# Feed-forward tiles of a two-layer decoder trunk placed at 192 instead of 64 bytes (mod 256) behind the weights

## The chip, the core and the metric

The kernel runs on one core of a Trainium2 chip. The core has a matrix engine (TensorE, PE in the profile, with PEld for the load of a matmul's stationary operand), a vector engine (VectorE, DVE), a scalar engine (ScalarE, ACT), GpSimd (POOL), and SyncE (SP), which here issues the DMAs. Tiles live in SBUF, 128 partitions wide; matmul results go to PSUM. The metric is the device time in microseconds of one execution of the whole program; lower is better. A matmul has a stationary operand, 128 x 128 here, that is loaded beforehand, and a moving operand of up to 512 columns that is streamed past it. The load for the next matmul runs while the present one streams.

## The reference

Two layers, each a mixer and a dense feed-forward part, with RMSNorm before and after each sub-layer. 256 positions, width 2048, hidden width 8192, float32. Cut to what the change is near:

```python
def squared_relu_mlp(h, w_up, w_down):
    return jnp.square(jax.nn.relu(h @ w_up)) @ w_down

def reference(x, norm_w, ...):
    h = x
    for layer in range(DEPTH):                       # 2
        y = rmsnorm(h, norm_w[layer, 0])
        y = linear_attention_mixer(y, ...) if layer % 2 == 0 else spatial_gating_mixer(y, ...)
        h = h + rmsnorm(y, norm_w[layer, 1])
        y = squared_relu_mlp(rmsnorm(h, norm_w[layer, 2]), ffn_w_up[layer], ffn_w_down[layer])
        h = h + rmsnorm(y, norm_w[layer, 3])
    return h
```

The first mixer is a gated DeltaNet beside a retention, the second a chunked gMLP (spatial gating).

## The kernel before

**Products in three parts.** Every large product is made with operands split into a high part (float32r) and a low part, the rest. `weights` (from L126 on) takes a 128 x 2048 tile of weights by DMA into `raw`, copies it to `whi` on ScalarE (L136) and writes the rest to `wlo` on VectorE (L137). Each product of a 128 x 128 block is then three matmuls: high x high, low x high, high x low.

**Who is stationary.** In `prod_tok` (L140, matmuls at L143 to L145) the activations are stationary and the weights move, 512 columns as a rule. In `up_pass` (L319, matmuls at L330 to L332) it is the other way round: a 128 x 128 piece of the weights is stationary and 256 columns of the normed activations, `xh` and `xl`, move. In `chunk7` (L361, matmuls at L374 to L376) the activations are stationary again and 256 columns of weights move.

**The feed-forward stage.** `ffn` (L389) runs twice, once per layer. The hidden width is cut into 16 chunks of 512. For chunk c the up projection is four quarters of 48 matmuls (`up_pass`, a generator that is advanced one quarter at a time); squared ReLU of the result is split into a pair of tiles `e` (high and low, 128 x 4 x 256 each), and sums and differences of its parts into a pair `f` (`sums`). Between the four quarters for chunk c, the down projection of chunk c-1 is done in four blocks, one for each 512 output columns, in the order of `ORDER` (L37): quarter, block 0, quarter, block 1, quarter, block 2, quarter, block 3. For c = 1 the order is `FIRST` (L38). A block (L439) for output columns 0 and 2 is done with seven products instead of eight (`chunk7`, a Strassen-like scheme, 42 matmuls of 256 columns with `e` and `f` stationary); block 1 is done so in every second pass and in the plain way in the others; block 3 is always plain. A plain block is 24 matmuls of 512 columns through `chunk_tok` and `prod_tok`, with `e` stationary. The first chunk (`first_chunk`) and the last one (`down_last`) are done by `prod_tok` too, the last one with `e` stationary. There are 15 passes in each of the two stages.

The tiles have two sets of names, `e0`, `f0` and `e1`, `f1`, used in turn by even and odd chunks; h and l at the end stand for high and low.

**Places.** The tile pools lie one behind the other in each partition of SBUF, and a tile's place follows from the sizes ahead of it. The tiles of `raw`, `whi` and `wlo` are 8192 bytes per partition each, and 128 bytes of padding ahead of them (`PAD0`, L33) put their start at 0 mod 256. The normed activations `xh` and `xl` are put at an offset within a larger tile (`group`, L206, with `X_IN` or `X_UP`, L34). In the trunk's mixers both start at 0 mod 256, in the feed-forward stages both at 64. The feed-forward tiles come from `pair` (L393): a filler of 64 bytes, the high tile of 4096 bytes, the low tile of 4096 bytes, a filler of 192 bytes. All other tiles of that pool are multiples of 256 bytes, so `e` and `f`, high and low, all start at 64 mod 256, and the slices that matmuls read start at multiples of 512 bytes behind that. The fillers are tiles of their own that GpSimd sets to zero once (`skip`, L114 to L116).

So in the two feed-forward stages, mod 256 bytes:

| block | matmuls | stationary operand | moving operand |
|---|---|---|---|
| quarter of the up projection (L330 to L332) | 48 of 256 columns | weights, at 0 | x, at 64 |
| seven-product block (L374 to L376) | 42 of 256 columns | e or f, at 64 | weights, at 0 |
| plain block (L143 to L145) | 24 of 512 columns | e, at 64 | weights, at 0 |

Elsewhere `prod_tok` has its stationary operand at 0, but for one pair of tiles in the first layer's output projection (`Um0`, `Um1`), which lies at 224; and in the first product of the first layer the moving slices are 400 columns, 1600 bytes, apart, so that slice j of a weight tile starts at 64 x j mod 256.

Of the kernel before, what the change touches and what calls it, by code (L numbers as in the profile page):

```python
# [96 lines left out]
def program(tc, nc, A, S):  # L97
# [16 lines left out]
    def skip(pool, n):  # L114
        uid[0] += 1
        G.memset(pool.tile([P, n // 4], F32, tag=f"skip{uid[0]}", name=f"skip{uid[0]}"), 0.0)  # L116

    def T(pool, shape, tag, dt=F32, bufs=None):
        uid[0] += 1
        kw = {} if bufs is None else {"bufs": bufs}  # L120
        return pool.tile(shape, dt, tag=tag, name=f"{tag}_{uid[0]}", **kw)
# [267 lines left out]
    def ffn(up, dn, X, rh, w1i, w0i):  # L389
        last = HID // 512 - 1  # L390
        with tc.tile_pool(name=f"ffn{w1i}", bufs=1, reuse_waits="tile") as fp:

            def pair(name):  # L393
                if name in seen:
                    return T(fp, [P, 4, SEQ], f"{name}h", F32R), T(fp, [P, 4, SEQ], f"{name}l", F32R)
                seen.add(name)
                skip(fp, 64)
                hi = T(fp, [P, 4, SEQ], f"{name}h", F32R)
                lo = T(fp, [P, 4, SEQ], f"{name}l", F32R)
                skip(fp, 192)  # L400
                return hi, lo

            seen = set()
# [11 lines left out]
            def sums(a, c):  # L415

                t = T(fp, [P, 1024], "tr")
                F = t.rearrange("p (i m t) -> p i m t", m=2, t=P)
                V.tensor_tensor(F[:, 0], a[1][0], a[1][1], ALU.subtract)
                V.tensor_tensor(F[:, 1], F[:, 0], a[0][0], ALU.subtract)  # L420
                V.tensor_tensor(F[:, 2], a[0][0], a[1][0], ALU.subtract)
                V.tensor_tensor(F[:, 3], F[:, 1], a[0][1], ALU.add)
                f = pair(f"f{c % 2}")
                split(f[0].rearrange("p a t -> p (a t)"), f[1].rearrange("p a t -> p (a t)"), t)
                return f

            def rows(c):
                return [c * 512 + j * P for j in range(4)]

            e = pair("e0")  # L430
            Y, kept = {}, [bank(acc, 512, "acc") for _ in range(2)]

# [50 lines left out]
            for c in range(1, last + 1):  # L483
                e2 = pair(f"e{c % 2}")
                if c == last:
                    w1 = row_load(rows_in(["f1h", "f1l"]), "nrow", w1i)
                ps = [bank(tpp, 512, "tp") for _ in range(2)]
                todo = up_pass(up, X, c, ps)
                order = ORDER if c > 1 else FIRST
                for n, o in enumerate(order):  # L490
                    if o is None:
                        next(todo)
                        if None not in order[n + 1 :]:
                            r = [relu2(p) for p in ps]
                            for i in range(2):
                                sl = slice(2 * i, 2 * i + 2)
                                split(e2[0][:, sl, :], e2[1][:, sl, :], r[i].rearrange("p (m t) -> p m t", t=SEQ))
                            if c < last:
                                a = [x.rearrange("p (m b t) -> p b m t", b=2, t=P) for x in r]
                                f2 = sums([[a[i][:, b] for i in range(2)] for b in range(2)], c)  # L500
                    else:
                        block(o, c - 1, e, f)
                e, f = e2, f2
# [668 lines left out]
```

## Time and profile before

| | us |
|---|---|
| median of 3 runs | 2483.79 (2483.1 to 2485.16) |
| the profiled execution | 2481.77 |
| its span, from the first to the last instruction | 2480.0 |
| first layer's mixer, about | 0 to 536 |
| first feed-forward stage, about | 536 to 1248 |
| gMLP mixer, about | 1248 to 1793 |
| second feed-forward stage, about | 1793 to 2480 |

A timeline row gives an instruction's start and duration in us. Matmuls overlap in the records: one of 256 columns is recorded with 278 ns on average while the next one starts long before that is over. The rate is read from the difference of two starts and the number of matmuls in between. An idle time stands only where the engine really had nothing to do. In the rows of the view by stretches, busy times of the engines stand in the order PE, PEld, DVE, ACT, POOL, each with the number of instructions.

### The profile page before, as it was taken

The numbers are of one execution on the slowest core, as the hardware profiler recorded it, in microseconds if no ns is written. First come the engines' busy times: TensorE is split into PE (matmuls) and PEld (weight loads), VectorE is DVE, ScalarE is ACT, GpSimd is POOL, SyncE is SP. The second block draws the span as 40 slices with busy tenths as digits, with TensorE's granted clock in tenths as the row PEclk, the third lists the DMA queues.
The fourth block names the chain that finished last, engine by engine and source line by source line (L and its number), as shares of the span: only waits on it lengthen the run. The fifth ranks groups of instructions, "written<-read, shape, count | busy, mean of one in ns | idle before, by whom it ended". The sixth has DMA issues, their size and how long they took to land.

```text
span 2480.0 us, 37131 instructions
## 1 busy us (share of the span) xinstructions
PE 2447.2 (99%) x15418; PEld 2191.0 (88%) x15418; DVE 1977.1 (80%) x2322; ACT 1261.5 (51%) x1266; POOL 185.4 (7%) x162
## 2 busy tenths in 40 slices
PE   9999999999999999999999999999999999999998
PEld 8878888879999999999878878888799999999997
DVE  6686855578898899889854596866888988988897
ACT  7655444455554555555553433333555546555553
POOL 0001201140000000000210120100400000000001
PEclk9999999999999999999999999999999999999999
DMA  8444545544555555555555555565445555555553
GB/s 315 158 164 141 192 161 177 207 170 179 212 188 194 214 202 190 188 207 216 193 215 187 186 202 201 200 221 203 153 170 206 202 187 216 194 194 194 204 208 133
DMA packets 81832, 480.17 MB, mean 194 GB/s; under 512 B 13696, under 2 KB 15872, under 8 KB 27392
## 3 DMA queue, kind: packets, MB, share of 16 engines
q1 hardware_dynamic: 81664, 477.80, 53.6%
q8 instruction: 121, 1.98, 0.3%
q14 instruction: 47, 0.39, 0.0%
HBM read 475.14 MB, written 2.62 MB: 193 GB/s over the span
## 4 chain that ended last, share of the span: by engine, by line
PE 46%; DVE 3%; POOL 1%; issue 1%; ACT 0%; DVEq 0%; POOLq 0%; ACTq 0%
PE acc L145 8%; PE acc L143 8%; PE acc L144 8%; PE tp L331 4%; PE tp L330 4%; PE tp L332 4%; PE acc L374 1%; PE acc L375 1%; PE acc L376 1%; PE mx L376 1%; PE mx L375 1%; PE mx L374 1%; DVE wlo L137 1%; DVE h L287 1%; PE mx L1082 1%
## 5 line engine op out<-in xcount | busy, mean ns | idle before, releaser
L137 DVE TENSOR_TENSOR wlo<-raw,whi 128x2048 fp32r<-128x2048 f32 (+3 forms) x366 | 825.2, 2257 | 254.0 <-ACT whi L136 249.7
L136 ACT ACTIVATE whi<-raw 128x2048 fp32r<-128x2048 f32 (+3 forms) x366 | 685.4, 1876 | 436.5 <-PE acc L144 274.7
L331 PE MATMUL tp<-xl,whi 128*128 128x256 f32 x1920 | 533.5, 278 | 0.0
L330 PE MATMUL tp<-xh,whi 128*128 128x256 f32 x1920 | 533.5, 278 | 0.0
L332 PE MATMUL tp<-xh,wlo 128*128 128x256 f32 x1920 | 533.3, 278 | 0.0
L143 PE MATMUL acc<-whi,xh 128*128 128x512 f32 (+3 forms) x1120 | 439.1, 392 | 3.5 <-ACT whi L136 3.5
L145 PE MATMUL acc<-wlo,xh 128*128 128x512 f32 (+3 forms) x1120 | 431.6, 387 | 1.3 <-DVE wlo L137 1.2
L144 PE MATMUL acc<-whi,xl 128*128 128x512 f32 (+3 forms) x1120 | 432.0, 386 | 0.0
L330 PEld LDWEIGHTS tp<-xh,whi 128*128 128x128 f32 x1920 | 360.6, 188 | 2.1
L331 PEld LDWEIGHTS tp<-xl,whi 128*128 128x128 f32 x1920 | 360.2, 188 | 1.9
L332 PEld LDWEIGHTS tp<-xh,wlo 128*128 128x128 f32 x1920 | 360.0, 188 | 0.0
L200 ACT ACTIVATE whi<-qsum 128x2048 fp32r<-128x2048 f32 x74 | 142.0, 1919 | 221.0 <-DVE qsum L355 210.8
L143 PEld LDWEIGHTS acc<-whi,xh 128*128 128x128 f32 x1120 | 211.0, 188 | 44.2 <-ACT whi L136 4.9
L145 PEld LDWEIGHTS acc<-wlo,xh 128*128 128x128 f32 x1120 | 210.5, 188 | 42.7 <-DVE wlo L137 2.4
L144 PEld LDWEIGHTS acc<-whi,xl 128*128 128x128 f32 x1120 | 211.0, 188 | 39.2 <-issue 1.0
L201 DVE TENSOR_TENSOR wlo<-qsum,whi 128x2048 fp32r<-128x2048 f32 x74 | 169.5, 2291 | 64.9 <-ACT whi L200 63.1
L200 ACT ACTIVATE whi<-raw 128x1536 fp32r<-128x1536 f32 x74 | 110.4, 1493 | 188.2 <-DMA raw<-dn 91.2
L201 DVE TENSOR_TENSOR wlo<-raw,whi 128x1536 fp32r<-128x1536 f32 x74 | 129.9, 1755 | 0.6 <-ACT whi L200 0.6
L446 DVE TENSOR_TENSOR y<-acc,y 128x512 f32<-128x512 f32 x136 | 92.4, 687 | 43.7 <-PE acc L376 43.7
L277 POOL TENSOR_TENSOR e0h<-y,f1h 128x512 f32<-128x512 f32 x8 | 13.1, 1653 | 1327.8 <-DVE y L275 1327.8
L145 PE MATMUL acc<-wlo,e0h 128*128 128x512 f32 x256 | 101.2, 395 | 0.0
L143 PE MATMUL acc<-whi,e0h 128*128 128x512 f32 x256 | 101.1, 395 | 0.0
(358 smaller groups left out, 4319.8 us busy)
## 6 DMA issues: line engine op xcount, KB each, us to landing
raw<-up SPq DMA_DIRECT2D x128, 1024.0 KB, 4.8
raw<-dn SPq DMA_DIRECT2D x128, 1024.0 KB, 4.8
raw<-sg_in SPq DMA_DIRECT2D x64, 1024.0 KB, 4.8
raw<-la_in SPq DMA_DIRECT2D x56, 1024.0 KB, 4.8
raw<-sg_out SPq DMA_DIRECT2D x32, 1024.0 KB, 4.8
raw<-la_out SPq DMA_DIRECT2D x16, 1024.0 KB, 4.7
raw<-la_in SPq DMA_DIRECT2D x4, 768.0 KB, 7.8
kq<-xT SPq DMA_DIRECT2D x8, 256.0 KB, 6.0
```

Of the source, the lines that this page charges most:

```text
L136: ACT.activation(a, r, AF.Copy)
L137: V.tensor_tensor(d, r, a.bitcast(F32), ALU.subtract)
L143: PE.matmul(ps, xh, wh, start=first, stop=False)
L144: PE.matmul(ps, xl, wh, start=False, stop=False)
L145: PE.matmul(ps, xh, wl, start=False, stop=last)
L200: ACT.activation(hi, src, AF.Copy)
L201: V.tensor_tensor(lo, src, hi.bitcast(F32), ALU.subtract)
L330: PE.matmul(out, wh[:, col], xh, start=k == 0 and m % 2 == 0, stop=False, skip_group_check=True)
L331: PE.matmul(out, wh[:, col], xl, start=False, stop=False, skip_group_check=True)
L332: PE.matmul(out, wl[:, col], xh, start=False, stop=k == NKT - 1, skip_group_check=True)
L374: PE.matmul(ps, x[k][0], wh, start=k == 0, stop=False, skip_group_check=True)
L446: V.tensor_tensor(Y[k, c], p, Y[k, c], ALU.add)
```

## The change

The two fillers of each pair swap their sizes. Each pair of tiles starts 128 bytes later within the same 8448 bytes, so `e` and `f` lie at 192 mod 256 instead of 64; everything behind a pair stays where it was. The normed activations stay at 64, the weights at 0. No instruction is added, removed or put elsewhere in an engine's order.

```diff
@@ pair, in ffn
                 seen.add(name)
-                skip(fp, 64)
+                skip(fp, 192)
                 hi = T(fp, [P, 4, SEQ], f"{name}h", F32R)
                 lo = T(fp, [P, 4, SEQ], f"{name}l", F32R)
-                skip(fp, 192)
+                skip(fp, 64)
                 return hi, lo
```

## The prediction

> **What bounds the kernel now.** I read the page's header and busy line first, then the slices, then the chain of work that ended last.
>
> ```profile
> span 2480.0 us, 37131 instructions
> PE 2447.2 (99%) x15418; PEld 2191.0 (88%) x15418; DVE 1977.1 (80%) x2322; ACT 1261.5 (51%) x1266; POOL 185.4 (7%) x162
> ...
> PEclk9999999999999999999999999999999999999999
> ...
> PE 46%; DVE 3%; POOL 1%; issue 1%; ACT 0%; DVEq 0%; POOLq 0%; ACTq 0%
> ```
>
> TensorE is busy 99% of the span, its granted clock never dips, and no other engine holds more than 3% of the chain. The busy time by stretches says the same of the two feed-forward stages, the only ones that the change touches:
>
> ```profile
> 700.00:900.00 200.00, 200.00 (x1592) 193.54 (x1591) 180.65 (x175) 106.50 (x78) 0.00 (x0) 1.00 0.55 196
> 2000.00:2200.00 200.00, 200.00 (x1560) 192.20 (x1559) 178.87 (x172) 108.77 (x85) 0.00 (x0) 1.00 0.54 194
> ```
>
> The columns after the stretch are its length, then busy time of PE, PEld, DVE, ACT and POOL, clock, DMA share, GB/s. PE is busy 200.00 of 200 us, VectorE 180.65. So only the rate at which matmuls follow one another can change here. A matmul's own duration doesn't show that rate, because matmuls overlap; the starts do. I therefore took the timeline of PE and read two whole passes of the feed-forward loop, where each block of matmuls begins (columns: start and duration in us, engine, line, operation, operands, shapes; in L374 and L143 the weights move and e is stationary, in L330 the weights are stationary and x moves):
>
> ```profile
> 700.91 0.29 PE L374 MATMUL acc<-whi,e1h 128*128 128x256 f32 x1
> 705.68 0.28 PE L330 MATMUL tp<-xh,whi 128*128 128x256 f32 x1
> 711.13 0.28 PE L374 MATMUL acc<-whi,e1h 128*128 128x256 f32 x1
> 716.08 0.28 PE L330 MATMUL tp<-xh,whi 128*128 128x256 f32 x1
> 721.73 0.28 PE L374 MATMUL acc<-whi,e1h 128*128 128x256 f32 x1
> 726.50 0.28 PE L330 MATMUL tp<-xh,whi 128*128 128x256 f32 x1
> 731.95 0.39 PE L143 MATMUL acc<-whi,e1h 128*128 128x512 f32 x1
> 737.53 0.28 PE L330 MATMUL tp<-xh,whi 128*128 128x256 f32 x1
> 743.19 0.29 PE L374 MATMUL acc<-whi,e0h 128*128 128x256 f32 x1
> 747.96 0.28 PE L330 MATMUL tp<-xh,whi 128*128 128x256 f32 x1
> 753.41 0.39 PE L143 MATMUL acc<-whi,e0h 128*128 128x512 f32 x1
> 759.00 0.28 PE L330 MATMUL tp<-xh,whi 128*128 128x256 f32 x1
> 764.65 0.29 PE L374 MATMUL acc<-whi,e0h 128*128 128x256 f32 x1
> 769.42 0.28 PE L330 MATMUL tp<-xh,whi 128*128 128x256 f32 x1
> 774.87 0.39 PE L143 MATMUL acc<-whi,e0h 128*128 128x512 f32 x1
> 780.46 0.28 PE L330 MATMUL tp<-xh,whi 128*128 128x256 f32 x1
> 786.11 0.29 PE L374 MATMUL acc<-whi,e1h 128*128 128x256 f32 x1
> ```
>
> An L330 block is a quarter of the up projection: 48 matmuls. An L374 block is a seven-product block: 42. An L143 block is an ordinary one with 512 columns: 24. Up blocks take either 5.45 us (705.68 to 711.13; 113.5 ns a matmul) or 5.65 us (716.08 to 721.73; 117.7 ns). Seven-product blocks take either 4.77 us (700.91 to 705.68; 113.6 ns) or 4.95 us (711.13 to 716.08; 117.9 ns). I call the two lengths short and long: 0.20 us apart for an up block, 0.18 us for a seven-product block. The 512-column block takes 5.58 us, 232.5 ns a matmul.
>
> The rows also give a rule of succession. After a 512-column block the up block is always long (737.53, 759.00, 780.46). A seven-product block takes the other length than the up block ahead of it: long up, short block (737.53, 743.19); short up, long block (705.68, 711.13). An up block keeps the length of the seven-product block ahead of it (711.13, 716.08). PE waits for nothing in there, so the two lengths are two ways in which the stream of moving columns and the load of the next stationary operand run beside each other, and something at the border passes one way on to the next block.
>
> **The change part by part.** Nothing is added to or taken from any engine's list: the memsets of 64 and 192 bytes swap places, no tile changes size, no DMA or wait moves. The memsets of all such fillers are this row, 1.3 us together on GpSimd, which is idle 93% of the span; that idle time hides them and I cost their swap at nothing (with no cover it couldn't exceed the 1.3 us):
>
> ```profile
> L116 POOL MEMSET skip<- 128x16 f32 (+2 forms) x18 | 1.3, 125 | 0.3 <-PE tp L219 0.3
> ```
>
> What moves is the place of e and f, read only as stationary operands. Call "relation" the place of the stationary operand less that of the moving one, mod 256 bytes. In an up block the weights (0) are stationary and x (64) moves: relation 192, unchanged. In the other two kinds e or f is stationary and the weights move: relation 64 now, 192 after. The single matmul at the border from up to block, with x moving while e is loaded, goes from relation 0 to 128; the one back stays at 0.
>
> *Term 1, the 512-column matmuls.* Their number comes from the groups kept apart by shape, one operation of three:
>
> ```profile
> L145 PE MATMUL acc<-wlo,e0h 128*128 128x512 f32 x256 | 101.2, 395 | 0.0
> L145 PE MATMUL acc<-wlo,e1h 128*128 128x512 f32 x176 | 69.3, 396 | 0.0
> ```
>
> (256 + 176) x 3 = 1296. Their cost at relation 192 isn't in this trace at 512 columns. The nearest rows are these. First the gMLP stage, relation 0, 24 matmuls; then a stationary tile that lies at 224, 11 matmuls; then matmuls of 400 columns in the first projection, where x is stationary at 0 and slice j of the weights begins at 64 x j, so that the relation is 192, then 128, then 64, six matmuls each (five counted of the last):
>
> ```profile
> 1306.54 0.39 PE L144 MATMUL acc<-whi,xl 128*128 128x512 f32 x1
> 1311.98 0.39 PE L144 MATMUL acc<-whi,xl 128*128 128x512 f32 x1
> ...
> 502.22 0.39 PE L143 MATMUL acc<-whi,Um 128*128 128x512 f32 x1
> 504.78 0.39 PE L145 MATMUL acc<-wlo,Um 128*128 128x512 f32 x1
> ...
> 23.03 0.34 PE L143 MATMUL acc<-whi,xh 128*128 128x400 f32 x1
> 24.12 0.34 PE L143 MATMUL acc<-whi,xh 128*128 128x400 f32 x1
> 25.22 0.34 PE L143 MATMUL acc<-whi,xh 128*128 128x400 f32 x1
> 26.14 0.34 PE L145 MATMUL acc<-wlo,xh 128*128 128x400 f32 x1
> ```
>
> Relation 0: 5.44 / 24 = 226.7 ns. Relation 224: 2.56 / 11 = 232.7 ns, as dear as the 232.5 of relation 64. At 400 columns: 1.09 / 6 = 181.7 ns at 192, 1.10 / 6 = 183.3 at 128, 0.92 / 5 = 184 at 64. The bounds are so from 0 (dear as now) to 232.5 - 226.7 = 5.8 ns saved, 7.5 us over 1296. I take the row that has the very relation, 184 - 181.7, about 2 ns: **-2.6 us**. I see no dearer relation among these rows than the present one, so the term gets no positive end.
>
> *Term 2, the lengths of the 256-column blocks.* Up blocks show that relation 192 has the same two lengths (113.5 and 117.7 ns) that relation 64 has in seven-product blocks (113.6 and 117.9). So I expect no new length, only another choice between the two, and that choice hangs on the border matmul, of which no row has relation 128 at 256 columns. The bounds come from counting. Each stage runs 15 passes, 7 pairs like the one above and a first pass; I count both stages as 15 pairs. A pair has 8 up blocks (4 long) and 5 seven-product blocks (1 long). All short: -(4 x 0.20 + 1 x 0.18) x 15 = -14.7 us. All long: +(4 x 0.20 + 4 x 0.18) x 15 = +22.8 us. Between these I take the count as it is, **0 us**: the levels mirror each other, and every row in which a 512-column block ends leads to the same long up block.
>
> *Sum.* -2.6 us on the profiled execution, 2481.77 us (span 2480.0 and 1.8 us around it): 2479.2. The median of the three runs is 2483.79, 2.0 us above the profiled one, so the forecast is 2483.79 - 2.6 = **2481.2 us**. What hides nothing: VectorE and ScalarE aren't late anywhere in these stretches, and 2.6 us spread over 1400 us of stages leaves VectorE's 90% as it is.
>
> **The rivals.**
>
> *Stuck long (slower).* With one relation throughout, the swap at the entry to the seven-product block may vanish. For: the swap occurs only where the relation changes from 192 to 64. Since each 512-column block leaves the long way behind, all blocks would then stay long until the next one, and the pass never gets out: 2483.79 + 22.8 - 2.6 = 2504.0 us. It decides from the first border matmul at relation 128: if an up block at 5.65 us is followed by a seven-product block at 4.95 us, this is it. Against: an undisturbed stream needn't hold its way over a border matmul with yet another relation.
>
> *Swap at the other border (slightly slower).* If what is passed on is a lag between the two streams, which the change of relation turns into the other length, then now the lag is kept on entry and turned over on return; without a change of relation the length would be kept on entry and swapped on return. The pass runs long up, long block, short up: up blocks as before, seven-product blocks 4 long of 5 for 1 of 5. 3 x 0.18 x 15 = +8.1, less 2.6: 2489.3 us. For: it needs no new behaviour at relation 128. Against: only two borders carry it.
>
> *Stuck short (faster).* As the first rival, but the 512-column block at its new relation leaves the short way behind: 2483.79 - 14.7 - 2.6 = 2466.5 us. Against: now it leaves the long way whichever way it was entered (from short at 726.50 and 747.96 alike), and the border behind it is unchanged.
>
> *Nothing at all.* The change may not touch the reads' rate: 2483.8 us. The rows speak against it, 226.7 against 232.5 ns for one shape with PE never idle, and only the place told apart. [...]
>
> **How the numbers follow.** Count as it is, term 1 alone (2481.2): 0.30. Swap at the other border (2489.3): 0.22. Stuck long (2504.0): 0.16. Stuck short (2466.5): 0.14. Nothing (2483.8): 0.08. Other mixes of lengths between the ends: 0.10. 0.2% is 5.0 us, about what a measurement of this kernel can tell from no change. Faster takes stuck short, a part of the forecast where term 1 comes nearer its far end of 7.5 us (0.10), and most of the mixes (0.08): 0.32. Slower takes stuck long, most of the other-border case (0.16; in the rest term 1 eats it below 5.0) and a little of the mixes (0.02): 0.34. Same: the remaining 0.34. Both signs are open. The forecast's own range is 2476 to 2484 by the ends of term 1; the range that should hold 8 times in 10 reaches from stuck short to stuck long, whose prices are exact if they come at all, since leaving either out would leave out a case whose chance I can't put far below the others': 2466 to 2505.
>
> **What would show it.** In the timeline of the changed kernel the same borders can be read. Term 1: a 512-column block from L143 to the next L330 should take about 5.53 us (5.58 less 24 x 2 ns). Term 2: up blocks 5.45 or 5.65, seven-product blocks 4.77 or 4.95, in the order of now. The gMLP stage and the first layer should keep their times. A third length (near 5.76 us for an up block, say) would make "no new length" wrong; a long seven-product block behind a long up block would show the swap gone; any growth of VectorE's or ScalarE's share on the chain would show that something else than PE's reads was touched.

## The result and the profile after

| | before | after |
|---|---|---|
| median of 3 runs, us | 2483.79 | 2502.56 (2499.51 to 2503.12) |
| ratio, with 95% interval | | 1.0071 [1.0057, 1.0085] |
| profiled execution, us | 2481.77 | 2499.51 |
| its span, us | 2480.0 | 2497.7 |

The change makes the kernel 0.7% slower. The forecast was 2481.2 us; the time lies near that of the first rival, *stuck long* (2504.0 us).

The page of the changed kernel shows nothing of it in its shares. These are its header, its busy line, the granted clock and the engines of the chain of waits:

```profile
span 2497.7 us, 37131 instructions
PE 2465.4 (99%) x15418; PEld 2213.8 (89%) x15418; DVE 1979.6 (79%) x2322; ACT 1260.8 (50%) x1266; POOL 185.5 (7%) x162
...
PEclk9999999999999999999999999999999999999999
...
PE 46%; DVE 3%; POOL 1%; issue 0%; ACT 0%; DVEq 0%; POOLq 0%; ACTq 0%
```

The instruction counts are those of before and the clock is full. VectorE and ScalarE have the work they had (1979.6 for 1977.1 us, 1260.8 for 1261.5); TensorE is busy 18.2 us longer, about as much as the span grew. The view by stretches says it in another way:

```profile
700.00:900.00 200.00, 200.00 (x1564) 193.98 (x1563) 178.54 (x173) 106.17 (x78) 0.00 (x0) 1.00 0.53 190
2000.00:2200.00 200.00, 200.00 (x1541) 192.98 (x1540) 174.20 (x166) 103.36 (x77) 0.00 (x0) 1.00 0.56 199
```

TensorE never idles, and yet only 1564 matmuls fall into the same 200 us where 1592 did, and 1541 for 1560. They follow one another more slowly. The timeline of TensorE over the same pair of passes, at the starts of the blocks (start and duration in us, then engine, line, operation and operands):

```profile
702.11 0.28 PE L374 MATMUL acc<-whi,e1h 128*128 128x256 f32 x1
707.05 0.28 PE L330 MATMUL tp<-xh,whi 128*128 128x256 f32 x1
712.71 0.28 PE L374 MATMUL acc<-whi,e1h 128*128 128x256 f32 x1
717.65 0.28 PE L330 MATMUL tp<-xh,whi 128*128 128x256 f32 x1
723.31 0.28 PE L374 MATMUL acc<-whi,e1h 128*128 128x256 f32 x1
728.25 0.28 PE L330 MATMUL tp<-xh,whi 128*128 128x256 f32 x1
733.91 0.39 PE L143 MATMUL acc<-whi,e1h 128*128 128x512 f32 x1
739.42 0.28 PE L330 MATMUL tp<-xh,whi 128*128 128x256 f32 x1
745.07 0.28 PE L374 MATMUL acc<-whi,e0h 128*128 128x256 f32 x1
750.01 0.28 PE L330 MATMUL tp<-xh,whi 128*128 128x256 f32 x1
...
788.59 0.28 PE L374 MATMUL acc<-whi,e1h 128*128 128x256 f32 x1
```

Every up block is long (707.05 to 712.71: 5.66 us) and so is every seven-product block (712.71 to 717.65: 4.94 us). The plain block became shorter, 5.51 us (733.91 to 739.42) for 5.58. The pair of passes takes 788.59 - 702.11 = 86.48 us; before it took 786.11 - 700.91 = 85.20. The difference times 15 pairs is 19.2 us, about the whole of the loss (18.8 us by the medians, 17.7 by the spans).

### The profile page after: what moved, and what is told of

It reads as the page before. It is cut to its first block, busy times and chain, and to the rows that moved or that the text cites. A ratio compares the mean times of both kernels' runs of the same rounds, so it can differ in the third digit from the quotient of the medians.

```text
span 2497.7 us, 37131 instructions
## 1 busy us (share of the span) xinstructions
PE 2465.4 (99%) x15418; PEld 2213.8 (89%) x15418; DVE 1979.6 (79%) x2322; ACT 1260.8 (50%) x1266; POOL 185.5 (7%) x162
## 4 chain that ended last, share of the span: by engine, by line
PE 46%; DVE 3%; POOL 1%; issue 0%; ACT 0%; DVEq 0%; POOLq 0%; ACTq 0%
PE acc L145 8%; PE acc L143 8%; PE acc L144 8%; PE tp L332 5%; PE tp L331 4%; PE tp L330 4%; PE acc L376 1%; PE acc L375 1%; PE acc L374 1%; PE mx L375 1%; PE mx L376 1%; PE mx L374 1%; DVE h L287 1%; DVE wlo L137 1%; PE mx L1082 1%
```

## The experiments

Theory A: the way in which a block of 256-column matmuls runs, short or long, is settled by the places that are read as one block passes into the next; with x at 64 and e at 192 that border leads to the long way. The rivals: another engine, or the order of products, does it; a place is dear by itself; only the relations of the two blocks count, and equal ones hand the way on (theory B).

**Matmuls alone.** A kernel that does only TensorE's part, on constant tiles, with no other engine at work. For each of 16 pairs of places (`px` for x, `pe` for e and f) it runs

```python
plain, plain, up, seven, up, plain, up, seven, up, seven, up, seven, up, plain
```

with the 24, 48 and 42 matmuls of the kernel's blocks.

> Leaves the whole computation out: only streams of matmuls on constant tiles, TensorE alone, for each of 16 pairs of places (x at 0, 64, 128, 192 by e at 0, 64, 128, 192) one even and one odd pass of the feed-forward loop, with up blocks of 48, seven-product blocks of 42 and plain blocks of 24 matmuls. Theory 'carried' (the two lengths belong to both relations, and the border decides which one goes on): x 64, e 64 repeats the order of before, up blocks 5.65 behind a plain block, then 4.77, 5.45; x 64, e 192 gives 5.65 and 4.95 everywhere; x 192, e 192 is the mirror of x 64, e 64 and swaps again, with 4.77 us blocks. Theory 'dear place' (a stationary operand at 192 is read slowly whatever came before): seven-product blocks 4.95 us for e at 192 whatever x is, 4.77 for e at 64 whatever x is. Theory 'other engines' (the lengths come from what ScalarE, VectorE and the DMAs do beside TensorE): all pairs alike, one length.

The timeline of this kernel, at the starts of the blocks from the second plain block's end on. First x and e at 64, then x at 64 and e at 192, then both at 192:

```profile
406.18 0.28 PE L46 MATMUL ps<-xh,whi 128*128 128x256 f32 x1
411.83 0.29 PE L46 MATMUL ps<-whi,eh 128*128 128x256 f32 x1
416.61 0.28 PE L46 MATMUL ps<-xh,whi 128*128 128x256 f32 x1
422.05 0.39 PE L46 MATMUL ps<-whi,eh 128*128 128x512 f32 x1
427.64 0.28 PE L46 MATMUL ps<-xh,whi 128*128 128x256 f32 x1
...
557.12 0.28 PE L46 MATMUL ps<-xh,whi 128*128 128x256 f32 x1
562.77 0.28 PE L46 MATMUL ps<-whi,eh 128*128 128x256 f32 x1
567.72 0.28 PE L46 MATMUL ps<-xh,whi 128*128 128x256 f32 x1
573.37 0.39 PE L46 MATMUL ps<-whi,eh 128*128 128x512 f32 x1
578.88 0.28 PE L46 MATMUL ps<-xh,whi 128*128 128x256 f32 x1
...
1163.70 0.28 PE L46 MATMUL ps<-xh,whi 128*128 128x256 f32 x1
1169.17 0.28 PE L46 MATMUL ps<-whi,eh 128*128 128x256 f32 x1
1173.93 0.28 PE L46 MATMUL ps<-xh,whi 128*128 128x256 f32 x1
1179.59 0.40 PE L46 MATMUL ps<-whi,eh 128*128 128x512 f32 x1
1185.19 0.28 PE L46 MATMUL ps<-xh,whi 128*128 128x256 f32 x1
```

At 64/64 the blocks take 5.65, 4.78, 5.44, 5.59 us: long up, short seven, short up, plain, as in the kernel before. At 64/192: 5.65, 4.95, 5.65, 5.51, all long, as in the changed kernel. So no other engine is needed. At 192/192: 5.47, 4.76, 5.66, 5.60. There e lies where the change put it, and the seven-product block is short; so 192 isn't dear in itself, and the rival of the dear place falls too. In this case the plain block leaves the *short* way behind, and the swap stands at the return border, seven to up.

**Both at 192 in the whole kernel.** The changed kernel, with x moved along:

```diff
-X_IN, X_UP = (0, 192), (64, 0)
+X_IN, X_UP = (0, 64), (192, 0)
```

(and the sizes of the two tiles in `group` exchanged, so that nothing behind them moves).

> x, e and f all at 192: the relations of up and down blocks are opposite again (64 and 192), the border matmul is at relation 0 as before. 'Carried': short and long blocks alternate as before, plain blocks near 5.51 us: about 2479 to 2484 us. 'Dear place': all seven-product blocks 4.95 us as after the change, 2495 to 2503 us.

2482.88 us against 2484.77 before on the same chip, ratio 0.9992 [0.9983, 1.0002]: no difference. 57 of the 114 up blocks whose 48 matmuls run without a break are long. The cost isn't in e's place but in the pair of places.

**Each half of the change alone.** `pair` skips 192 for names that begin with f and 64 for the others, and the other way round.

> Half of the change: f alone at 192, e stays at 64. Within a seven-product block the relation then changes from 64 (12 matmuls) to 192 (24) and back (6), with x moving or standing nowhere between. 'Carried', with the swap made by the change of relation itself: the f part has the other length than the e part, about 2483 to 2492 us. 'Carried', with the swap made by the border matmul of relation 0 alone: no change within the block, 2484 us. 'Dear place': the f part is long in every block, 58 blocks x 24 x 4.4 ns = 6 us more, about 2490 us.

> The other half: e alone at 192, f stays at 64. The border from an up block is at relation 128 as after the change, plain blocks at relation 192 (5.51 us). 'Carried': the e part at the start of a seven-product block keeps the long way of the up block, and if a change of relation swaps, the f part is short, the last e part long again: up blocks all long, 2483.8 + 12 (up) - 4 (plain) + about 1 = near 2493 us; if only a border of relation 0 swaps, all long, 2502 us. 'Dear place': up blocks as before, e parts long: 2484 to 2488 us.

f alone: 2483.26 us in one run, within the range of the kernel before on that chip (2482.38 to 2487.16). A short seven-product block stays short through its four products on f (744.14 to 746.86: 2.72 us for 24 matmuls); a long one stays long there (722.58 to 725.40: 2.82 us), and only its last product, back at e, is short (725.40 to 726.08: 0.68 us for 6). e alone: 2489.51 us in one run, 4.7 us over the median of before on that chip; 74 of 114 up blocks are long. In this trace the products on e right behind an up block are long whichever way the up block ran (behind one of 5.66 us, 714.36 to 715.77: 1.41 us for 12 matmuls); the products on f, going from 192 to 64, in some blocks become short (748.13 to 750.86: 2.73 us) and in others stay long (715.77 to 718.60: 2.83 us). By these single runs there is no cost without e, and e alone brings about a quarter of it. The up block hands over to e; but the rest of the loss needs f at 192 too, since with f at 64 the products on f turned short in 40 of the 72 seven-product blocks, and each time the up block behind them was short.

**The border alone, on matmuls alone.** 26 cases in the order of an even and an odd pass. In some, only the last matmuls of an up block read x at another place; in others one product of the seven reads at another place.

> The second kernel of matmuls alone: it leaves the whole computation out and writes one tile of sums to the output. Up, seven-product and plain blocks on constant tiles, in the order of an even and an odd pass, for 26 choices of places. Theory A, the border matmul's own relation decides (128 leads to the long way from either way, 0 turns one way into the other at the entry from up to seven): with x at 64 and e at 192, reading x at 192 in the last matmul of an up block alone makes the border relation 0, and seven-product blocks behind a long up block become short (113.3 ns a matmul for 117.8); with x and e at 64, reading x at 192 in that one matmul makes the border 128, and all blocks of the pass become long. Theory B, only the relations of the two blocks count (equal ones keep the way): the first case stays all long, the second keeps today's alternation. A way out, by the first map's rows where an up block with x at 192 was short behind a seven-product block with e at 0 (113.3 ns) and behind any plain block at 192: x and e at 192 with only the last product of the seven (6 matmuls) at 0 should make all up blocks short, 113.3 ns, and the seven-product blocks short but for those 6 matmuls. If the ways depend on more than the border, these up blocks alternate as they do with all places at 192 (long before each plain block).

Theory A's sharp form fell here. With x at 64 and e at 192, one matmul that reads x at 192 (border relation 0) gave now short and now long blocks. The last three matmuls doing so gave today's alternation throughout, 85.21 us a pair of passes for the 86.48 of all long blocks. With x and e at 64, one matmul at 192 made all blocks long but for one seven-product block and the up block behind it. So what is read at the border does decide, but not by the border relation of one matmul. How many matmuls it takes differs with the places: with x and e at 192, the very last matmul of the seven products at 0 was enough to make every up block short (84.01 us a pair). Theory B, for which these cases were to stay as they were, falls. The way out came as expected: x and e at 192, the last product of the seven at 0, gave 84.18 us a pair with every up block short (113.7 to 113.9 ns a matmul). The same with x at 64, e and f at 192 and the *first* product at 0: 84.67 us; there only up blocks behind a plain block are long.

**First tries in the whole kernel.** The product on the first part of f is moved to the front of the seven (`entry0`) or to their end (`exit0`, with x at 192), and that part is put at 0; the split of f is done in two instructions each on ScalarE and VectorE.

```diff
+        prod(pc[:, :256], summed(R1), q1)
         prod(pa[:, :256], plain(0, 0), b11)
...
-                split(f[0].rearrange("p a t -> p (a t)"), f[1].rearrange("p a t -> p (a t)"), t)
+                split(f[0][:, :256], f[1][:, :256], t[:, :256])
+                split(f[0][:, 304:], f[1][:, 256:], t[:, 256:])
```

> A control: the changed kernel (x at 64, e and f at 192) with the seven-product block's first product now the one on the first part of f, and the split of f done in two instructions each; all operands stay at 192. Theory A (the places read at the border decide): border relation still 128, everything stays long, 2502 us. If the order of the products or the time at which f is ready matters, it departs from that.

> As entry192, but the high half of the first part of f lies at 0 mod 256, so that the first product of each seven-product block (4 of its 6 matmuls) reads at 0; everything else stays at 192. Theory A: the border from a long up block is no longer at relation 128 between two streams of relation 192, so the seven-product blocks turn short (113 to 114 ns a matmul), and so do the up blocks behind them; the second map gave 84.67 us for the 16 blocks of a pair of passes where all at 192 gave 86.48, so 1.81 x 15 = 27 us less than entry192: about 2475 us. Theory B (equal relations keep the way): 2502 us plus 148 x 4 x some 3 ns = 2504 us.

> x, e and f all at 192; the product on the first part of f comes last in the seven-product block, and its high half lies at 0 mod 256 (the low half at 192). By the second map, up blocks behind a seven-product block that ends at 0 are short, and those behind a plain block at 192 too (113.7 to 113.9 ns): all 59 up blocks and all 37 seven-product blocks of a stage short, plain blocks near 229 ns. 84.18 us a pair for the 85.20 of the order that alternates as before does: 15 x 1.0 = 15 us less than before, about 2468 us, more if the plain blocks reach 229 ns all through. If the ways in the whole kernel are set by more than the places at the borders: 2483, as x192_e192.

> As exit0, with the low half of the first part of f at 0 too, so that all 6 matmuls of the last product read at 0 (512 bytes more of the pool). Theory A: the same borders as exit0, 2 more matmuls of 42 at up to 120 ns for 113.3, at most 74 x 2 x 6.7 ns = 1 us more than exit0. If it is the single last matmul and not the product that counts, the same within a microsecond.

All four missed: 2515.88, 2518.97, 2506.9 and 2507.19 us, ratios 1.0126 and 1.0136 for the first two and 1.0089 and 1.0091 for the others. The edit did more than move a place. VectorE and ScalarE have 30 instructions more each, and the work on TensorE came out in another order: 88 up blocks run without a break, where 114 did. (The kernels further down move products and add no such instruction; there it is 114 again.) From the timeline of `exit0`:

```profile
724.59 0.28 PE L374 MATMUL acc<-whi,e1h 128*128 128x256 f32 x1
730.23 0.28 PE L330 MATMUL tp<-xh,whi 128*128 128x256 f32 x1
730.69 0.39 PE L143 MATMUL acc<-whi,e1h 128*128 128x512 f32 x1
730.92 0.28 PE L332 MATMUL tp<-xh,wlo 128*128 128x256 f32 x1
736.11 0.40 PE L144 MATMUL acc<-whi,e1l 128*128 128x512 f32 x1
```

The up block at 730.23 is interrupted after 4 matmuls by one matmul of the plain block, and the seven-product block in front takes 5.64 us, more than the long way of 4.95, since it waits for its weights (TensorE waits at L376 for them 16 times in this run, 8.1 us together). So the times say nothing of theory A. The blocks do say something. In `exit0`, where only the high half of that part lies at 0 (4 of the last 6 matmuls, the very last among them), 43 of the 88 up blocks without a break are short, and only 15 of the 46 right behind an unbroken seven-product block. In `exit0b`, with all 6 at 0, it is 87 of 88, and all 46. At the entry it is alike: in `entry0`, with 4 of the first 6 matmuls at 0, 54 of the 56 unbroken seven-product blocks without a recorded idle time still ran long. That goes against what theory A expected of `entry0`. In the whole kernel a product that reads at 0 in only one of its halves wasn't enough, although the matmul at the border was one of those at 0.

**The way out, with no instruction added.** Two of f's four parts are put at 0 by a gap *within* the tile, so that one split instruction still writes it. The two products that read them come last (the order is now the three products on e, then R2, R3, S4, R1). x and e are at 192. `exit192_f` is the control with the same order and no gap.

```diff
-                split(f[0].rearrange("p a t -> p (a t)"), f[1].rearrange("p a t -> p (a t)"), t)
+                split(f[0], f[1], t.rearrange("p (a t) -> p a t", a=2))
...
+                    t.append(T(fp, [P, 2, 560], f"{name}{k}", F32R)[:, :, :512])
```

> x, e and f at 192, and two of the four parts of f, used by the last two products of each seven-product block, at 0 (by a gap inside the tile; no instruction added, the split stays one instruction each, the order on TensorE by blocks is that of before). Both halves of those parts are at 0, as in the second map's case with the last product at 0. Theory A: all 118 up blocks behind a seven-product block that ends at 0 or behind a plain block at 192 are short, 60 x 48 x 4.4 ns = 12.7 us less; seven-product blocks 30 x 113.3 + 12 x some 119 ns, mean 115, for a mean of 114.4 before: 74 x 42 x 0.6 = 2 us more; plain blocks 229 to 233 ns: 0 to 5 us less. Together about 2469 to 2474 us. Theory B (only the relations of whole blocks count): about 2483.

> The control: the same order of products and of the parts of f, everything at 192. Both theories: as x192_e192, the blocks alternate and the time is that of before, 2483 to 2485 us.

> The changed kernel (x at 64, e and f at 192) with the first two products of each seven-product block on two parts of f that lie at 0, and no instruction added or displaced. Theory A: the border from the up block is at relation 192 against the up block's 192, the seven-product blocks turn short behind it (30 x 113.3 + 12 x some 119) and so do the up blocks behind them; only up blocks behind a plain block stay long: 2502.6 less 70 x 48 x 4.4 ns = 15 us and less 74 x 42 x 2.7 ns = 8 us, about 2479 us. Theory B: 2503.

`exit0_f`: 2467.72 us, ratio 0.9939 [0.9922, 0.9956]. The control: 2479.6, 0.9984 [0.9974, 0.9993], and 58 of 114 up blocks long. It is about 4 us under what was expected; its blocks take in sum what they took before, and where those 4 us come from stays open. In `exit0_f` all 114 up blocks are short; the places alone, against the control, are worth 2479.6 - 2467.72 = 11.9 us. Its timeline, up block, the products at 192, those at 0, up block; then, one round later, up to plain to up:

```profile
702.95 0.29 PE L330 MATMUL tp<-xh,whi 128*128 128x256 f32 x1
708.41 0.28 PE L374 MATMUL acc<-whi,e1h 128*128 128x256 f32 x1
711.81 0.28 PE L374 MATMUL mx<-whi,f1h 128*128 128x256 f32 x1
713.25 0.29 PE L330 MATMUL tp<-xh,whi 128*128 128x256 f32 x1
...
723.55 0.29 PE L330 MATMUL tp<-xh,whi 128*128 128x256 f32 x1
729.01 0.39 PE L143 MATMUL acc<-whi,e1h 128*128 128x512 f32 x1
734.50 0.28 PE L330 MATMUL tp<-xh,whi 128*128 128x256 f32 x1
739.97 0.28 PE L374 MATMUL acc<-whi,e0h 128*128 128x256 f32 x1
```

Up blocks 5.46 us, also behind the plain block (734.50 to 739.97: 5.47). The thirty matmuls at 192 of a seven-product block take 3.40 us, 113.3 ns each; the twelve at 0 take 1.44, 120 ns each, a dear stretch that pays for the short up block behind it. The plain block takes 5.49.

`entry0_f` missed: 2513.71 us for 2479, 1.0122 [1.0107, 1.0137]. In it the two products moved to the front need the weight sums that ScalarE and VectorE split last. TensorE waits for them there, 15.0 us in 29 waits. The view by stretches (length, busy PE, PEld, DVE, ACT, POOL, granted clock, DMA share, GB/s):

```profile
745.00:750.00 5.00, 3.19 (x28) 2.99 (x26) 3.36 (x5) 2.38 (x2) 0.00 (x0) 1.00 0.21 26
...
752.00:753.00 1.00, 1.00 (x7) 1.00 (x6) 0.66 (x1) 1.00 (x2) 0.00 (x0) 0.50 0.65 270
...
755.00:760.00 5.00, 5.00 (x47) 5.00 (x46) 5.00 (x5) 1.92 (x1) 0.00 (x0) 1.00 0.45 159
```

TensorE is busy 3.19 of 5 us, and a little later its granted clock is at 0.50, with 7 matmuls in that us for 47 in the 5 us from 755 on, where the clock is full again. Breaks and slow matmuls within the unbroken blocks (counted where two starts lie over 1.3 times their block's median apart) add up to some 29 us over both stages, for none in the kernel before. So its time says nothing of theory A either; but in 28 of the 35 unbroken seven-product blocks without a recorded idle time the products at 192 ran short, as theory A has it.

**The changed kernel's own border.** What was still missing: the border of the change undone in the whole kernel, with no product moved and the lists of TensorE, VectorE and ScalarE as they are. The gap now goes into the tile of e. `entry0_e` puts the half that the first product reads at 0, `second0_e` the other half (with eight more small fillers that GpSimd sets). The edit of `entry0_e`:

```diff
+                    a = T(fp, [P, 2, 560], f"{name}{k}", F32R)[:, :, :512]
+                    if name + k not in seen:
+                        skip(fp, 128)
```

> The changed kernel (x at 64, f at 192), with the first half of each e tile at 0 and the second half at 192, by a gap in the tile; no instruction is added and no product moved, so that VectorE's and ScalarE's lists are those of the changed kernel. The first of the seven products then reads at 0, the other six at 192; in a plain block the first 12 matmuls read at 0, the last 12 at 192. Theory A (what is read at the border decides): the six products at 192 turn short and the up blocks behind a seven-product block too; those behind a plain block stay long. Against the changed kernel: 74 x 48 x 4.4 ns = 15.6 us from up blocks, 74 x (36 x 4.4 - 6 x 2) ns = 10.8 us from seven-product blocks, 54 x 12 x 2.3 ns = 1.5 us from plain ones: 2502.6 - 28 = about 2475 us. Theory B (only the relations of whole blocks count, or the cost is a matter of other engines): no change but the 1.5 us, 2501.

> The mirror control of entry0_e: the first half of e at 192, the second half at 0, else the same. The border from up to seven-product block is again at relation 128, so if only that border decides, nothing turns short: 2502.6 us, plus 74 x 12 x 2.2 ns = 2 us, less 1.5 us in the plain blocks: about 2503 us. If it is a stretch at relation 0 in front of one at 192 that sets the short way, wherever it stands, the four products between the two at 0 turn short and the up blocks stay long: 74 x 24 x 4.4 ns = 7.8 us less, about 2495 us.

`entry0_e`: 2475.68 us, 0.9964 [0.9952, 0.9977]; theory A had expected about 2475. `second0_e`: 2502.47, 1.0075 [1.006, 1.009]; expected were about 2503. First a few blocks of `entry0_e` (up, the first product at 0, the six at 192, up), then of `second0_e` (first product at 192, second at 0, four at 192, last at 0, up):

```profile
706.73 0.28 PE L330 MATMUL tp<-xh,whi 128*128 128x256 f32 x1
712.17 0.28 PE L374 MATMUL acc<-whi,e1h 128*128 128x256 f32 x1
712.89 0.28 PE L374 MATMUL acc<-whi,e1h 128*128 128x256 f32 x1
716.97 0.28 PE L330 MATMUL tp<-xh,whi 128*128 128x256 f32 x1
722.41 0.28 PE L374 MATMUL acc<-whi,e1h 128*128 128x256 f32 x1
```

```profile
714.18 0.28 PE L374 MATMUL acc<-whi,e1h 128*128 128x256 f32 x1
714.89 0.28 PE L374 MATMUL acc<-whi,e1h 128*128 128x256 f32 x1
715.61 0.28 PE L374 MATMUL mx<-whi,f1h 128*128 128x256 f32 x1
718.44 0.28 PE L374 MATMUL mx<-whi,e1h 128*128 128x256 f32 x1
719.15 0.28 PE L330 MATMUL tp<-xh,whi 128*128 128x256 f32 x1
724.81 0.28 PE L374 MATMUL acc<-whi,e1h 128*128 128x256 f32 x1
```

In the first, 36 matmuls at 192 take 4.08 us (712.89 to 716.97), 113.3 ns each, and the up blocks 5.44. In the second, 24 matmuls at the same place take 2.83 us (715.61 to 718.44), 117.9 ns each, and the up block 5.66. Both kernels mix the places 0 and 192, with the same f at 192; what differs is which half of e lies where, and with it what the up block hands over to. (The last product of the seven, and the halves of the plain blocks, differ too; but the 24 matmuls compared here run ahead of that last product.) All 72 up blocks behind an unbroken seven-product block are short in the one, none in the other. That a stretch at 0 ahead of one at 192 is enough by itself, the second kernel refutes.

## Why the prediction was wrong

- *What bounds the kernel*: right. Only the rate of the matmuls changed; VectorE, ScalarE, DMA and clock stayed as they were.
- *No new length*: right for the changed kernel. Up blocks take 5.66 us and seven-product blocks 4.94, the long ones of before.
- *Term 1*, the 512-column matmuls: the direction was right, the size too small. 5.51 us for 5.58 is 0.07 / 24 = 2.9 ns a matmul, 3.8 us over 1296, where the 400-column rows had given 2 ns and 2.6 us. That the sign came right was luck in part, since the relation doesn't settle this cost by itself: on matmuls alone the plain block at 192 takes 5.51 us when entered from a long up block with x at 64, and 5.60, no less than before, when entered from a long one with x at 192.
- *Term 2*, "the count as it is, 0 us": this is the step that failed. The ground for it was that the levels mirror each other and that every plain block leads to the long up block. Both hold, but they don't settle what the border at relation 128 does, and the text said itself that no row has it. In its place the runs showed the upper bound, "all long", +22.8 us: of the blocks without a break, 114 of 114 up blocks are long for 58 before, and 72 of 72 seven-product blocks for 16. In the two traces these up blocks grew by 11.7 us together and these seven-product blocks by 9.5. With term 1 as measured, 22.8 - 3.8 = 19.0 us; the medians differ by 18.8.
- *Stuck long*: this rival came about, in its course and its price. Its sign, a long seven-product block behind a long up block, is what the timeline shows. Its reason, that the swap may vanish where the relation no longer changes, is not enough. On matmuls alone the mirrored pair (x at 192, e at 64, both relations 64) doesn't stay stuck: its seven-product block behind a long up block is short in `map16`. So equal relations alone don't do it. Nor does the border matmul's relation alone, which is 128 in that case too.
- *Swap at the other border*: not for this change; but it is what x and e at 192 do, where the seven-product block keeps the up block's way and the up block behind it swaps (5.47, 4.76, 5.66 us in `map16`).
- *Stuck short*: not for this change. `exit0_f` shows such a state from other places, with 148 x 6 = 888 matmuls at 120 ns as its price. That its 2467.72 us lies near the 2466.5 of that rival is chance in part, since its control is some 4 us faster than expected, for a reason that stays open.
- *Nothing at all*: refuted. The change moved places alone and cost 18.8 us. With every other engine quiet, the same 48 matmuls took 5.44 or 5.65 us at the same places (`map16`, x and e at 64), by what ran before.

Open stays why there are two ways at all. That they are two ways in which the moving columns and the load beside them run was the author's estimate from the two lengths: no view shows what happens between a moving read and the load beside it. What tells a border that swaps from one that keeps is known here only case by case.

## What to carry to other kernels

Where TensorE is busy all the time and its clock is full, compare the starts of equal blocks: here the two lengths of one shape, 5.44 and 5.65 us for 48 matmuls of 256 columns, went with the operands' places and their sequence. Try places in pairs, stationary against moving, and over the borders between blocks: here e and f at 192 cost 18.8 us with x at 64, and with x at 192 the time was that of before (ratio 0.9992). A cheap kernel of matmuls alone in the real order gave the pattern for 16 pairs in one run of 1401.97 us. Then change places by gaps and fillers alone: here added instructions changed the order of the work on TensorE, and products moved to the front made it wait (15.0 us in `entry0_f`), and either buried an effect of half a per cent.

## What the runs showed of the hardware that was not expected

- One stream of 256-column matmuls with 128-column loads, at the same places, ran at about 113.4 or 117.8 ns a matmul, in the kernel before through whole blocks (56 and 58 of the 114 up blocks without a break); on matmuls alone what ran just before picked the one. In `map16` with both operands at 0, every block of 256-column matmuls but the first of the run took about 120 ns a matmul, as dear as any seen there. Of its 512-column blocks those with both at 0 were the cheapest, from 226.7 ns, against 228.8 to 233.9 for stationary operands at the other multiples of 32.
- The last matmuls of a block settled the way of the whole next block in some cases. In the whole kernel, with x and e at 192 and 6 of the last 6 matmuls at 0, all 46 up blocks behind unbroken seven-product blocks were short (`exit0b`); with 4 of 6, 15 of 46 (`exit0`). On matmuls alone the last one at 0 was enough (`map26`, 84.01 us a pair); why the whole kernel asked for more is not shown.
- In `entry0_f`, an idle time of 2.2 us on TensorE was followed by a granted clock of 0.57, 0.50, 0.50 and 0.72 in the four us from 751 to 755, which makes about 3.4 us at 0.50. Not every such idle time was: behind one of 2.26 us in the first layer, up to 126.01 us, the clock stood at 1.00 in the kernel before, and so it did behind one of 2.28 us, up to 126.95 us, in the changed one.
